# A two-layer trunk kernel rescheduled: idle products at its start, an embedding unit among the last heads, and half chunks split ahead from three tiles

## The chip, the cores and the metric

The kernel runs on one core of one Trainium2 chip. The metric is the time on the device in microseconds (us), as a median of several runs; less is better. TensorE does the matrix products (PE in the profile, its weight loads PEld), VectorE (DVE) and ScalarE (ACT) do elementwise work, GpSimd (POOL) a little, and SyncE (SP) issues the DMAs in its program order. Every engine works through its own instructions in order, and waits on semaphores for the others.

## What is computed (the reference)

Two decoder layers work on 1024 tokens of width 1024. Layer 0 mixes tokens by gated linear attention (GLA, 4 heads, chunks of 64 in the reference), layer 1 by sparse attention: an indexer of 8 small heads scores all keys, the best 256 for each query are kept, and 16 heads attend to those alone. After the mixer come a layer norm and a gated embedding. Cut to what matters:

```python
for i in range(DEPTH):                       # DEPTH = 2
    y = gla_mixer(x, ...) if i == 0 else dsa_mixer(x, ...)
    x = layer_norm(ALPHA * x + y, ln_g[i], ln_b[i])
    x = x + (p[i] @ ple_w[i]) * jax.nn.sigmoid(x @ ple_gate_w[i])

# gla_mixer                                  # dsa_mixer, for a block of 128 queries
h = x @ w_in          # q, k, v, z, a          score = sum over heads of relu(qi . ki) * wi
g = log_sigmoid(a @ w_a2 + b_a) / 16           idx = top_k(where(causal, score, -inf), 256)
G = cumsum(g)                                  probs = softmax(q . k[idx] * scale)
o = tril(q e^G . k e^-G) v + state term        o = probs @ v[idx]
y = (rmsnorm(o) * gn_g * silu(z)) @ w_out      y = (o * silu(z)) @ w_out
```

All of it is in fp32.

## The kernel before

**Products.** An fp32 product of a weight block and an activation block is made as three products of rounded parts: high by high, low by high, high by low. So every operand that TensorE reads exists as a high part (rounded by ACT) and a low part (the difference, by DVE). One product is 128x128 weights by 512 columns and goes through `mm` (L58). Which line helpers have: `split` is L403 (high, ACT) and L395 (low, DVE).

**Weights.** `Weights` holds the list of weight blocks (128x1024) in the order in which they are used. A block is loaded into a `wst` tile (L199; two of these), and split in four steps: `whi` for its two halves on ACT (L180), `wlo` on DVE (L182, or L184 with a factor). Blocks that were split earlier are loaded as `whi` and `wlo` from DRAM (L167). Steps are taken as TensorE's work is emitted, or at the latest when `take` asks for the block.

**Splitting ahead.** In the first 1030 us, the background generator `split_ahead` (L203) takes 65 weight blocks of layer 1 in 130 halves of 128x512 through: load into `pst` (L210; two tiles), high part `phi` on ACT (L219; one tile), store `whs` (L221), low part on DVE in place (L223), store `wls` (L225). The load of the next half stands on SP ahead of the store of this one's low part.

**Order of the work.** `Flow` is a clock at build time: each product adds its nominal time, and other work is put on a heap with a due time (`at`, `after`, `chain`, `spread`) or given out by three `Background` generators with a gap between steps. What is due is emitted between products. So the numbers in the code are emission times, and what they fix is the order of each engine's instructions and nothing else.

**Stages.** Both layers are gone through in two halves of 512 tokens.
- Layer 0 (until about 1030 us): for each half, four heads. `v_phase`, gates (`g_phase`: log-sigmoid as Exp then Ln on ACT, L513 and L514, then a scan on DVE, L521, and exponentials), `qk_phase`, the state recurrence, and the output products of the head before (`out_phase`). Then `tail` (L816): 8 blocks of embedding products, transposes of the normed `y`, 8 gate blocks. In half 0 follow the parts of layer 1 that need only these tokens: `small_head` (indexer's projections, tile `zz`), `small_kv` (keys, values), the indexer's scores (`ix`, `rl` L1022, `sc` L1018), and the loads of half 1's `x` (L1138).
- Layer 1: the first half begins with the same small parts of half 1. Then 16 heads, each with one or two units of other products beside it (queries `q`, gates `z`, output blocks `o`); the softmax's parts `ph` and `PT` (L1481, L1479) feed the `o` products. In half 0 the top-k searches of the later query blocks run beside the heads, as a background of counting passes (`tk<-sc,tki`, L1040 on DVE, L1084 on ACT). After head 15 come `last_outs`, three output units: (6, column half 1), (7, 0), (7, 1). The last two need `u` of head 15, which is `uf` = `o` times `z` (L1533), split by ACT and DVE. Then `norm_steps` (L789) and `tail` again.

The few lines which set what the change touches:

```python
chain((0, lambda: None), (0.6, soft(0)), (1.1, soft(1)), (0.3, scan(0)), (1.1, scan(1)), ...)   # g_phase
bg3.set(W.split_ahead(later, lp), 2.1)                    # half 0, the first head
bg3.due = max(bg3.due, fl.now + 14.0)                     # after small_head
bg.set(topk_steps([4, 5, 6, 7], scs, l1, tk, tk, on_act=(1, 2, 3)), 1.6)
```

## Time and profile before

| | |
|---|---|
| runs before | 2016.35, 2017.49, 2019.79 us; median 2017.49 |
| the profiled execution | its own time 2016.59 us; its span, from the first instruction to the last, 2014.8 us, so 1.8 us lie around the span |
| granted TensorE clock, mean | 0.993 |
| DMA | 464.96 MB, mean 231 GB/s; 16 engines busy 68.4% of the span by packets of the main queue |
| chain that ended last | PE 81%, DVE 7%, ACT 5%, DMA 4%, issue 2% |

The rows in the section below come from one profiled execution. A row of the timeline is: start in us, busy us, engine, line, operation, output<-inputs, tile shape, count, and in brackets how long the engine sat idle just before and what ended that. "DVE", "ACT" and "PE" are busy times; a matmul's busy time includes its pipeline, so products that follow each other closely overlap in their rows. A row of the waits is: who waited for whom, us in total, how often, the longest. A row of the windows is: the stretch, its length, busy time (and instructions) of PE, PEld, DVE, ACT, POOL, then the granted clock of TensorE (1 is full), the DMA engines' share and GB/s.

### The profile page before, as it was taken

Reading aid. Unit: us, or ns where it says so; the run is one execution under the profiler, and the core shown is the slowest. Engines: PE = TensorE matmul, PEld = TensorE weight load, DVE = VectorE, ACT = ScalarE, POOL = GpSimd, SP = SyncE. Lnnn points to the kernel's source line nnn. Section 1 sums busy time; section 2 is a strip of 40 time slices with the busy share of each in tenths; the row PEclk is TensorE's granted clock in tenths of the full one; section 3 lists DMA queues with packets and bytes.
Section 4 is the critical chain, followed back from the end, with each engine's and each line's share of the span. In section 5 each row is a group of like instructions: output and inputs, shape, how many; then the busy total and the mean of one; then the engine's idle time right before and its main releaser. Section 6 shows DMA issues by size and latency. Waiting matters only on the chain.

```text
span 2014.8 us, 26716 instructions
## 1 busy us (share of the span) xinstructions
PE 1963.4 (97%) x9016; PEld 1616.3 (80%) x9016; DVE 1487.6 (74%) x3037; ACT 1046.5 (52%) x1943; POOL 53.7 (3%) x111
## 2 busy tenths in 40 slices
PE   8999999999999999999999999999899999999999
PEld 6788788877777888888888887888778888888877
DVE  5667666687677797877867986777796887777863
ACT  5664646445465646464555676766442553434432
POOL 0000000010000000000100000000000000000000
PEclk9999999999999999999999999999999999999999
DMA  4557575657856565657667487877766998888864
GB/s 149 174 162 221 171 218 171 222 174 243 283 180 224 161 225 167 225 162 224 196 218 266 157 311 246 303 265 276 271 211 215 352 333 295 291 300 279 295 249 147
DMA packets 173947, 464.96 MB, mean 231 GB/s; under 512 B 20081, under 2 KB 20849, under 8 KB 167665
## 3 DMA queue, kind: packets, MB, share of 16 engines
q1 hardware_dynamic: 173808, 463.25, 68.4%
q8 instruction: 71, 1.16, 0.2%
q14 instruction: 68, 0.55, 0.1%
HBM read 331.18 MB, written 131.99 MB: 230 GB/s over the span
## 4 chain that ended last, share of the span: by engine, by line
PE 81%; DVE 7%; ACT 5%; DMA 4%; issue 2%; SPq 0%; POOL 0%; POOLq 0%; ACTq 0%; DVEq 0%
PE pb L58 59%; PE o L58 8%; PE U L58 6%; PE S L58 5%; DMA xst<-x2s 1%; DMA wls<-pst 1%; DMA pst<-in_d_o 1%; DVE bn L803 1%; PE oT L62 1%; PE tr L58 1%; DVE wlo L182 1%; DVE sc L1018 1%; ACT whi L180 0%; DMA wst<-in_g_v 0%; DMA wlo<-wls 0%
## 5 line engine op out<-in xcount | busy, mean ns | idle before, releaser
L58 PE MATMUL pb<-x,whi 128*128 128x512 f32 x2272 | 709.9, 394 | 3.3 <-ACT whi L180 2.0
L58 PEld LDWEIGHTS pb<-x,whi 128*128 128x128 f32 x2272 | 417.2, 188 | 84.4 <-ACT whi L180 2.8
L58 PE MATMUL pb<-x,wlo 128*128 128x512 f32 x1136 | 444.2, 391 | 0.4 <-DVE wlo L182 0.4
L58 PE MATMUL pb<-whi,u 128*128 128x512 f32 x1024 | 347.2, 399 | 7.6 <-DVE u L395 4.2
L58 PEld LDWEIGHTS pb<-x,wlo 128*128 128x128 f32 x1136 | 213.8, 188 | 48.1 <-DVE wlo L182 2.3
L58 PEld LDWEIGHTS pb<-whi,u 128*128 128x128 f32 x1024 | 194.8, 190 | 49.9 <-DVE u L395 5.0
L58 PE MATMUL pb<-wlo,u 128*128 128x512 f32 x512 | 202.3, 395 | 0.0
L182 DVE TENSOR_TENSOR wlo<-wst,whi 128x512 fp32r<-128x512 f32 x232 | 154.8, 684 | 56.2 <-ACT whi L180 56.0
L180 ACT ACTIVATE whi<-wst 128x512 fp32r<-128x512 f32 x232 | 136.4, 621 | 47.2 <-DMA wst<-in_g_z 13.7
L219 ACT ACTIVATE phi<-pst 128x512 fp32r<-128x512 f32 x130 | 81.4, 626 | 126.2 <-DMA pst<-in_d_z 40.8
L1435 ACT ACTIVATE sq<-P,mx 128x128 f32<-128x128 f32 (+7 forms) x128 | 99.0, 774 | 83.8 <-DVE mx L1428 56.5
L1481 ACT ACTIVATE ph<-PT 128x512 fp32r<-128x512 f32 (+1 forms) x160 | 93.7, 601 | 65.7 <-PE o L58 50.4
L58 PE MATMUL S<-kT,q 128*128 128x512 f32 (+2 forms) x576 | 121.8, 343 | 0.0
L1479 DVE TENSOR_TENSOR PT<-PT,ph 128x512 fp32r<-128x512 f32 (+1 forms) x160 | 101.5, 648 | 20.6 <-ACT ph L1481 20.6
L58 PEld LDWEIGHTS S<-kT,q 128*128 128x128 f32 x576 | 100.6, 188 | 17.8 <-DVE mx L1428 0.7
L58 PEld LDWEIGHTS pb<-wlo,u 128*128 128x128 f32 x512 | 97.6, 191 | 18.8
L223 DVE TENSOR_TENSOR pst<-pst,phi 128x512 fp32r<-128x512 f32 x130 | 89.1, 685 | 29.8 <-ACT phi L219 29.8
L1084 ACT ACTIVATE tk<-sc,tki 128x768 f16<-128x768 f32 (+2 forms) x90 | 92.9, 1032 | 22.0 <-DVE tki L1093 15.9
L58 PE MATMUL o<-ph,vT 128*128 128x512 f32 (+2 forms) x384 | 102.4, 351 | 0.0
L1441 DVE STREAM_TRANSPOSE sq<-sq 128x128 f32<-128x128 f32 (+7 forms) x128 | 97.6, 768 | 3.1 <-ACT sq L1435 3.0
L58 PE MATMUL pb<-whi,x 128*128 128x512 f32 x256 | 89.1, 407 | 10.0 <-ACT whi L180 6.0
L709 ACT ACTIVATE junk<-o 128x512 bf16<-128x512 f32 x32 | 19.1, 597 | 139.8 <-DVE ot L707 135.3
(311 smaller groups left out, 3383.9 us busy)
## 6 DMA issues: line engine op xcount, KB each, us to landing
whi<-whs SPq DMA_DIRECT2D x130, 512.0 KB
wlo<-wls SPq DMA_DIRECT2D x130, 512.0 KB
sqd<-sq SPq DMA_DIRECT2D x192, 256.0 KB
PT<-sqd SPq DMA_DIRECT2D x48, 1024.0 KB
whs<-phi SPq DMA_DIRECT2D x130, 256.0 KB
wls<-pst SPq DMA_DIRECT2D x130, 256.0 KB
wst<-in_g_v SPq DMA_DIRECT2D x32, 512.0 KB
wst<-in_g_z SPq DMA_DIRECT2D x32, 512.0 KB
```

The source lines that it names most:

```text
L58: self.pe.matmul(out, lhsT, rhs, start=start, stop=stop)
L62: self.pe.transpose(out, in_, ident)
L180: self.nc.scalar.activation(hi[:, c], st[:, c], AF.Copy, scale=1.0 if gain is None else gain)
L182: self.nc.vector.tensor_sub(lo[:, c], st[:, c], hi[:, c].bitcast(F32))
L219: self.nc.scalar.activation(hi, st.bitcast(F32), AF.Copy)
L223: self.nc.vector.tensor_sub(st, st.bitcast(F32), hi.bitcast(F32))
L803: dve.bn_stats(st8[:, t, c], y[:, t, c * 512:c * 512 + 512])
L1084: act.activation(junk()[:, :n], scs[j], AF.Sign, bias=cand[:, j:j + 1].bitcast(F32), accum_out=cnt[:, j:j + 1])
L1435: act.activation(to, rows, AF.Exp, scale=-1.0, bias=mx, accum_out=sm[:, t:t + 1])
L1441: dve.transpose(x, x)
L1479: dve.tensor_sub(lo, lo.bitcast(F32), hi.bitcast(F32))
L1481: chain((0, lambda: act.activation(hi, lo.bitcast(F32), AF.Copy)), (0.8, second))
```

## The change

1. **Start.** 22 products `ident` by `ident` (128x128, fp32, result unused) stand ahead of TensorE's first product. The first block's four split steps and the split of the first `x` block are emitted one after the other, then the rest.
2. **Gates.** `g_phase` takes Exp of both halves, then Ln of both; the scans are put 2.2 us later and 0.7 us apart.
3. **Splitting ahead.** Three `pst` tiles, and the loads run two halves ahead instead of one; `phi` takes turns in the two `xst` tiles of another pool; gap 2.06 instead of 2.1. From the start of `small_head`, the generator is held for seven blocks (35.8 us by the build clock), so nothing of it stands beside the indexer's blocks; before, it was held for 14 us after `small_head`.
4. **Half 1's `x`** is loaded by its own generator during `small_head`, two blocks each 5 us, and is split later and more slowly (from block 12 of `small_kv`, gap 2.2). The first weights of half 1 (`in_g_v`) are no longer tied to these loads.
5. **Layer 0's end of a half.** The inputs of the embedding are staged in the `e1` tile and split 7 us later.
6. **Norm.** The statistics of the first 512 columns are taken as soon as these are complete; the apply step comes at 1.8 instead of 2.0.
7. **Layer 1's end of a half.** Two of the eight embedding blocks (12 products) become a unit of `last_outs` between (6, 1) and (7, 0), with weights in the `wst` tiles; the tail does the other six. `z` times `inv` is taken one group earlier. In half 1, head 15's `o` products are packed into 4.2 us. The embedding's inputs are loaded at head 14 instead of head 15, and the searches pause 5 us after head 15's last group.
8. **Searches.** Gap 1.52 (was 1.6), and in the heads' slots 1.75 or 1.5.

The diff's core:

```diff
     def split_ahead(self, keys, pool, hi_pool):
...
-            st = pool.tile([128, 512], F32R, tag="pst", name="pst", bufs=2)
+                tiles[i] = pool.tile([128, 512], F32R, tag="pst", name="pst", bufs=3)
...
+        load(0)
+        load(1)
...
-            hi = pool.tile([128, 512], F32R, tag="phi", name="phi")
+            hi = hi_pool.tile([128, 512], F32R, tag="xst", name="phi", bufs=2)
...
-            nxt = load(*cuts[i + 1]) if i + 1 < len(cuts) else None
+            load(i + 2)
...
-    last_outs = [("o", (6,), 1), ("o", (7,), 0), ("o", (7,), 1)]
+    last_outs = [("o", (6,), 1), ("p",), ("o", (7,), 0), ("o", (7,), 1)]
...
+        def exps():
+            for d in range(2):
                 act.activation(ta[:, d], ta[:, d], AF.Exp, scale=-1.0)
+
+        def logs():
+            for d in range(2):
                 act.activation(ta[:, d], ta[:, d], AF.Ln, bias=1.0)
...
+            fl.need(lambda: X.t[0] is not None)
+            for _ in range(4):
+                W.step()
             next(feeder)
             feed_by(feeder, 0.0, 0.0)
+            idle = pp.tile([128, 512], F32, tag="o", name="o")
+            for _ in range(22):
+                nc.tensor.matmul(idle[:, 0:128], ident, ident, start=True, stop=True)
...
-                    bg3.set(W.split_ahead(later, lp), 2.1)
+                    bg3.set(W.split_ahead(later, lp, xp), 2.06)
...
+            nxt = start_half(1)
+            feed_by(nxt[3], fl.now + 2.0, 5.0)
+            bg3.due = max(bg3.due, fl.now + 7 * B)
             fl.run(small_head(0, X, f32t, alloc, lambda: t2k("u", F32R), tmp, ups, kih, kil, res))
...
-            bg3.due = max(bg3.due, fl.now + 14.0)
-            nxt = start_half(1)
-            next(nxt[2])
...
+                if g == len(groups) - 2:
+                    z, inv = get(("z", h), ("inv", h))
+                    dve.tensor_mul(z, z, inv)
+                    st["zs", h] = z
                 if last:
-                    dve.tensor_mul(z[0], z[0], z[1])
...
-        bg.set(topk_steps([4, 5, 6, 7], scs, l1, tk, tk, on_act=(1, 2, 3)), 1.6)
+        bg.set(topk_steps([4, 5, 6, 7], scs, l1, tk, tk, on_act=(1, 2, 3)), 1.52)
...
+    def ple_unit(st):
+        st["pw"] = W.take(("p", 1, 0))
+        st["ple"] = [small_tile("qf") for _ in range(2)]
+        for b in range(2):
+            yield from ple_block(st["pw"], b, Pt, st["ple"][b], act)
...
+            bg.gap = 1.75 if h > 3 and h % 4 < 2 else 1.5
```

What that does to the order of the instructions is shown at three places.

**ACT, the gates of the first head** (`z` is a block of the output gate, `ta` the gate's halves). Before:

```order
L602 ACT_TABLE_LOAD
L602 ACTIVATE z<-pb 128x512
L513 ACT_TABLE_LOAD
L513 ACTIVATE ta<-ta 128x512
L514 ACT_TABLE_LOAD
L514 ACTIVATE ta<-ta 128x512
L180 ACTIVATE whi<-wst 128x512
L513 ACT_TABLE_LOAD
L513 ACTIVATE ta<-ta 128x512
L514 ACT_TABLE_LOAD
L514 ACTIVATE ta<-ta 128x512
```

The same place after the change:

```order
L610 ACT_TABLE_LOAD
L610 ACTIVATE z<-pb 128x512
L519 ACT_TABLE_LOAD
L519 ACTIVATE ta<-ta 128x512 x2
L181 ACTIVATE whi<-wst 128x512
L523 ACT_TABLE_LOAD
L523 ACTIVATE ta<-ta 128x512 x2
```

Four table loads for a head's Exp and Ln have become two; the weights' `whi` stands between the pairs.

**SP, the indexer's blocks of half 0** (`in_x_T` is half 1's raw `x`, `in_g_v` its first weights, `in_d_q` a half to be split ahead). Before:

```order
L225 DMA wls<-pst 128x512
L221 DMA whs<-phi 128x512
L210 DMA pst<-in_d_q 128x512
L1138 DMA y<-in_x_T 128x512
L199 DMA wst<-in_g_v 128x1024
L1138 DMA y<-in_x_T 128x512
L199 DMA wst<-in_g_v 128x1024
L1138 DMA y<-in_x_T 128x2x512 x3
L963 DMA v<-rope_s 32x512
L964 DMA v<-rope_s 32x512
L199 DMA wst<-in_g_v 128x1024 x2
L225 DMA wls<-pst 128x512
```

After:

```order
L1160 DMA y<-in_x_T 128x2x512
L168 DMA whi<-whs 128x1024
L168 DMA wlo<-wls 128x1024
L1160 DMA y<-in_x_T 128x2x512
L985 DMA v<-rope_s 32x512
L986 DMA v<-rope_s 32x512
L200 DMA wst<-in_g_v 128x1024 x3
L230 DMA wls<-pst 128x512
L200 DMA wst<-in_g_v 128x1024
L226 DMA whs<-phi 128x512
L214 DMA pst<-in_d_q 128x512
```

The loads of `x` stand apart and ahead of the weights, and no `phi` or `pst` stands between them and `in_g_v`.

**PE and SP, the end of layer 1's half 0** (`o` are head 15's last groups, `pb<-whi,u` output products, `pb<-q,wst` the embedding unit, `sc` the indexer's scores of the query blocks that are still searched). PE before:

```order
L58 MATMUL o<-PT,vT_9801 128x4x96
L58 MATMUL pb<-whi,u 128x512
L58 MATMUL pb<-wlo,u 128x512
L58 MATMUL pb<-whi,u 128x512
L58 MATMUL o<-ph,vT_9801 128x4x64
L58 MATMUL o<-ph,vT_9802 128x4x64
L58 MATMUL o<-PT,vT_9801 128x4x64
L58 MATMUL o<-ph,vT_9801 128x4x64
L58 MATMUL o<-ph,vT_9802 128x4x64
L58 MATMUL o<-PT,vT_9801 128x4x64
L58 MATMUL pb<-whi,u 128x512
L58 MATMUL pb<-wlo,u 128x512
```

PE after:

```order
L58 MATMUL o<-PT,vT_9821 128x4x96
L58 MATMUL pb<-q,wst 128x512 x3
L58 MATMUL o<-ph,vT_9821 128x4x64
L58 MATMUL o<-ph,vT_9822 128x4x64
L58 MATMUL o<-PT,vT_9821 128x4x64
L58 MATMUL o<-ph,vT_9821 128x4x64
L58 MATMUL o<-ph,vT_9822 128x4x64
L58 MATMUL o<-PT,vT_9821 128x4x64
L58 MATMUL pb<-q,wst 128x512 x6
L58 MATMUL pb<-whi,u 128x512
L58 MATMUL pb<-wlo,u 128x512
```

SP before:

```order
L1507 DMA inv<-row 128x512
L1077 DMA sc_9809<-sc_s 128x768
L167 DMA whi<-whs 128x1024
L167 DMA wlo<-wls 128x1024
L1077 DMA sc_9810<-sc_s 128x896
L1077 DMA sc_9811<-sc_s 128x1024
```

SP after:

```order
L1099 DMA sc_9829<-sc_s 128x768
L1536 DMA inv<-row 128x512
L1099 DMA sc_9830<-sc_s 128x896
L168 DMA whi<-whs 128x1024
L168 DMA wlo<-wls 128x1024
L1099 DMA sc_9831<-sc_s 128x1024
```

In place of the first three output products, embedding products stand between the last `o` groups, and six more behind the last. The scores of 896 keys are loaded ahead of a pair of weight blocks instead of behind it.

More of the change, by code (lines that the diff above doesn't have):

```diff
@@ L163, in step @@
                 self.loads(n + 1)
-            self.parts[n] = tuple(self.pool.tile([128, 1024], F32R, tag=t, name=t, bufs=4) for t in ("whi", "wlo"))
+            tags = (("wst", 2),) * 2 if self.seq[n][0][:3] == ("p", 1, 0) else (("whi", 4), ("wlo", 4))
+            self.parts[n] = tuple(self.pool.tile([128, 1024], F32R, tag=t, name=t, bufs=b) for t, b in tags)
         if whole:
@@ L773, in out_phase @@
             parts = [W.take(("o", u["h"], ch, 0)), W.take(("o", u["h"], ch, 1))]
-            for i, _ in enumerate(accumulate(parts, U, y, ch, u["rs"], norm if ch else None)):
+            for i, _ in enumerate(accumulate(parts, U, y, ch, u["rs"], norm)):
                 if ch:
@@ L810, in apply, with ple_block, tail @@
                 f_done[t] = True
-            chain((0, stats), (2.0, apply))
+            if ch:
+                chain((0, stats), (1.8, apply))
         return norm, f_done
-    def tail(layer, Pt, y, y_done, final, tp, xps, x_alloc, tmp):
-        ple = [tp.tile([128, 4, HT], F32, tag="z", name="ple", bufs=2) for _ in range(2)]
+    def ple_block(parts, b, Pt, out, engine):
+        hi, lo = parts
+        ps = pbank()
+        n = 0
+        for k in range(2):
+            ph, pl = Pt[k]
+            bs = slice(k * 512 + b * 128, k * 512 + b * 128 + 128)
+            for l, r in ((hi, ph), (hi, pl), (lo, ph)):
+                mm(ps, l[:, bs], r, n == 0, n == 5)
+                n += 1
+            if k == 0:
+                yield
+        if engine is dve:
+            dve.tensor_copy(out, ps)
+        else:
+            act.activation(out, ps, AF.Copy)
+        yield
+    def tail(layer, Pt, y, y_done, final, tp, xps, x_alloc, tmp, ple=(), first=None):
+        ple = list(ple)
+        done = len(ple)
+        for c in range(2):
+            t = tp.tile([128, 4, HT], F32, tag="z", name="ple", bufs=2)
+            ple += [t[:, i] for i in range(4)]
         X1 = [None] * NK
@@ L1138, in load, with fetch @@
             nc.sync.dma_start(raw[:, k:k + n], x_T[k:k + n, :, hs].rearrange("k p t -> p k t"))
+        def fetch():
+            for k in range(0, NK, 2):
+                load(k, 2)
+                yield
         def feed():
-            load(0, 1)
-            W.loads(W.ns + 1)
-            load(1, 1)
-            W.loads(W.ns + 2)
-            for k in range(2, NK, 2):
-                load(k, 2)
-            if half == 0:
+            if half == 0:
+                load(0, 1)
+                W.loads(W.ns + 1)
+                load(1, 1)
+                W.loads(W.ns + 2)
+                for k in range(2, NK, 2):
+                    load(k, 2)
                 nc.sync.dma_start(ba, g_ba)
@@ L1151, in feed @@
                 nc.sync.dma_start(fq, freq)
-            else:
-                yield
             for k in range(NK):
@@ L1512, in f @@
             def f():
-                (ph, pl), *z = get(("parts", h, g), *([("z", h), ("inv", h)] if last else []))
+                (ph, pl), = get(("parts", h, g))
                 fl.req(not first or st.get("done", -1) == h - 1, not last or h < 5 or st["out"] >= h - 4)
@@ L1644, in trunk_kernel @@
                 spread(parts[early:], start + lead + early * step, dur - lead - 2.4 - early * step)
-                spread(pvs, start + lead + 2.9, dur - lead - 2.4)
+                if h == 15 and half:
+                    spread(pvs, start + 8.6, 4.2)
+                else:
+                    spread(pvs, start + lead + 2.9, dur - lead - 2.4)
             if h < 15:
```

112 lines of the change are left out of this document (52 added, 60 removed).

## The prediction

> **What bounds the kernel now.** I read the page's first parts, then the windows by stage, the waits of TensorE, and the timeline around each window in which TensorE idles.
>
> ```profile
> PE 1963.4 (97%) x9016; PEld 1616.3 (80%) x9016; DVE 1487.6 (74%) x3037; ACT 1046.5 (52%) x1943; POOL 53.7 (3%) x111
> ...
> 0.00:12.43 12.43, 5.47 (x11) 3.71 (x12) 5.93 (x14) 7.72 (x13) 2.37 (x12) 1.00 0.76 264
> ...
> 405.00:425.00 20.00, 17.95 (x81) 14.54 (x80) 15.25 (x26) 9.43 (x23) 1.79 (x6) 0.91 0.32 105
> ...
> 530.00:566.00 36.00, 29.77 (x117) 22.90 (x116) 31.07 (x56) 22.82 (x43) 0.00 (x0) 0.91 0.65 220
> ...
> 630.00:650.00 20.00, 16.79 (x73) 13.75 (x73) 14.00 (x34) 7.34 (x16) 0.75 (x2) 0.91 0.82 289
> 650.00:1220.00 570.00, 564.88 (x2632) 466.49 (x2631) 460.36 (x985) 325.71 (x612) 19.23 (x39) 1.00 0.63 210
> 1220.00:1240.00 20.00, 17.84 (x76) 14.37 (x75) 14.58 (x36) 11.22 (x25) 0.00 (x0) 0.91 0.77 282
> ...
> 1440.00:1462.00 22.00, 15.87 (x63) 12.49 (x62) 14.68 (x27) 3.87 (x7) 0.00 (x0) 0.84 0.80 281
> ...
> 1930.00:1950.00 20.00, 17.94 (x72) 14.07 (x71) 13.75 (x24) 4.62 (x9) 0.39 (x2) 0.91 0.65 256
> ```
>
> TensorE is busy 97% of the span, and its products are what the work consists of: in 650 to 1220 it idles 5.12 us of 570. So only three things can be won: the first 6 us, the holes, and the clock. Six short stretches hold nearly all of that. Their idle time is 20 - 17.95 = 2.05, 36 - 29.77 = 6.23, 20 - 16.79 = 3.21, 20 - 17.84 = 2.16, 22 - 15.87 = 6.13 and 20 - 17.94 = 2.06 us. In each, the granted clock is below 1, and I looked for where:
>
> ```profile
> 411.79:415.20 3.41, 3.41 (x12) 2.75 (x11) 3.14 (x6) 0.00 (x0) 0.00 (x0) 0.50 0.27 71
> ...
> 1452.85:1459.68 6.83, 4.24 (x10) 3.37 (x11) 5.35 (x10) 0.00 (x0) 0.00 (x0) 0.50 0.73 258
> 1940.96:1944.37 3.41, 3.41 (x8) 2.76 (x9) 1.43 (x3) 0.00 (x0) 0.00 (x0) 0.50 0.00 0
> ```
>
> Behind each hole lies a window of 3.41 us at half clock; these three rows stand for seven such stretches, of which the second holds two windows. One in which TensorE is busy throughout costs at most 3.41 / 2 = 1.7 us. There are two in 530 to 566 and two in 1440 to 1462 (there with 4.24 us busy, so 2.1 us together). What is to be had at most is thus 3.8, 9.6, 4.9, 3.9, 8.2 and 3.8 us: 34.2 in all, and the start.
>
> **The change part by part.** *Start.*
>
> ```profile
> 1.09 0.23 DVE L356 TENSOR_SCALAR ident<-negs 128x128 f32<-128x128 int32 x1 [1.09 <-POOL negs L354]
> ...
> 5.98 0.79 PE L58 MATMUL pb<-whi,x 128*128 128x512 f32 x1 [5.98 <-ACT whi L180]
> ...
> 7.74 1.29 DVE L395 TENSOR_TENSOR x<-y,x 128x512 fp32r<-128x512 f32 x2
> ...
> 9.92 1.05 PE L58 MATMUL pb<-whi,x 128*128 128x512 f32 x2
> ...
> 10.78 0.63 PE L58 MATMUL pb<-wlo,x 128*128 128x512 f32 x1
> ...
> 12.46 0.39 PE L58 MATMUL pb<-whi,x 128*128 128x512 f32 x1
> ...
> 12.69 0.40 PE L58 MATMUL U<-whi,x 128*128 128x512 f32 x1
> ...
> 15.45 0.39 PE L58 MATMUL pb<-whi,x 128*128 128x512 f32 x1
> ...
> 95.89 0.45 PE tr L58 x4
> ```
>
> The first weight block's 24 products last from 5.98 to 15.45. Three take 10.78 - 9.92 = 0.86 us until 12.43, that is, 0.43 each (though this window's row says 1.00, so I take the slow pace from the products), and 0.23 behind it. The idle products can begin at 1.32, when `ident` is there. 128x128 products of this kind take 0.45 / 4 = 0.112 us (last row); 22 at half pace take 4.9 us and end at about 6.3, no later than the first product's operands by more than 0.3. If the pace is full by 9, the sixth product, which needs `x` 1's low part at about 8.9 (DVE's second half of the row at 7.74, behind two `wlo`), is what comes last. The 18 behind it then take 18 x 0.23 = 4.1, and end at 13.0: 2.4 us gained. If it stays slow until 12.43, 0.7.
>
> *Gates.*
>
> ```profile
> L513 ACT ACT_TABLE_LOAD x16 | 20.5, 1283 | 0.3
> ...
> PE pb L58 <- DVE m L509: 3.0, 6, 0.8
> ```
>
> There are as many for Ln at L514, and half of the 32 go: 16 x 1.283 = 20.5 us of ACT, which is 52% busy, so nearly all of it lies beside TensorE's work. What TensorE feels is its wait for the gates, 3.0 us in six times. I take 2.0 (0 to 3.0), and with the start 4.4.
>
> *405 to 425.* TensorE waits for `Al`, the low part of the chunk's scores:
>
> ```profile
> 407.15 0.62 ACT L219 ACTIVATE phi<-pst 128x512 fp32r<-128x512 f32 x1
> ...
> 407.81 0.69 DVE L223 TENSOR_TENSOR pst<-pst,phi 128x512 fp32r<-128x512 f32 x1 [1.84 <-ACT phi L219]
> ...
> 411.34 0.50 PE L58 MATMUL o<-v,Al 128*128 128x512 f32 x1 [2.05 <-DVE Al L395]
> ```
>
> A half's `phi` stands on ACT just ahead of `Ah`, and its `pst` ahead of DVE's queue that ends in `Al`. With other gaps, they stand behind: 0.62 + 0.69 of the 2.05 us go, likely the window with it. I take 2.8 (0 to 3.8).
>
> *530 to 566.* The indexer's blocks:
>
> ```profile
> 542.08 1.15 ACT L180 ACTIVATE whi<-wst 128x512 fp32r<-128x512 f32 x2 [4.27 <-DMA wst<-in_g_v]
> ...
> 543.66 0.62 PE L58 MATMUL ix<-v,u 128*128 128x384 f32 x2 [2.51 <-ACT rl L1022]
> ...
> 561.54 0.75 PE L62 MATMUL U<-ident,zz 128*128 128x128 f32 x4 [2.81 <-ACT zz L984]
> ```
>
> ACT waits 4.27 us at a weight half that was issued among the loads of `x`; `rl` and TensorE behind it stop for 2.51. The loads of `x` now lie earlier and apart, nothing else is ahead of the weights, and that hole closes with its window. The second, 2.81, comes from DVE, which is busy 31.07 of these 36 us; one `x` split (0.69) more or less stands there, and a `pst` has come into it. I take 5.0 (2.5 to 8.0).
>
> *630 to 650.* A `phi` holds ACT:
>
> ```profile
> ACT phi L219 <- DMA pst<-in_d_z: 40.8, 19, 4.1
> ...
> 633.28 0.33 SPq L210 DMA_DIRECT2D pst<-in_d_o  x1
> ...
> 637.08 0.63 ACT L219 ACTIVATE phi<-pst 128x512 fp32r<-128x512 f32 x1 [3.29 <-DMA pst<-in_d_o]
> ...
> 637.74 0.69 DVE L223 TENSOR_TENSOR pst<-pst,phi 128x512 fp32r<-128x512 f32 x1 [1.81 <-ACT phi L219]
> ...
> 639.09 0.49 PE L58 MATMUL tr<-ta,m 128*128 128x128 f32 x2 [3.21 <-DVE m L589]
> ```
>
> The load lands 3.8 us after its issue, the `phi` waits 3.29 at the head of ACT, DVE 1.81 behind it, TensorE 3.21 behind that. ACT's next `whi` stands behind that `phi` too. A load now comes a whole half earlier, three steps of 2.06 = 6.2 us, which covers 3.29. On SP it stands between the same two stores as before and waits for the same one (the low part of the half before), so nothing queued behind it waits longer; the `phi` waits for the store of the last but one instead of the last. I take 4.4 (0, if SP is what holds the load, to 4.9).
>
> *1220 to 1240.* Here, DVE does a counting pass and its search step between the operands and `PT`:
>
> ```profile
> 1225.41 0.84 DVE L1040 TENSOR_SCALAR_CACHE_REDUCE tk<-sc,tki 128x640 f16<-128x640 f32 x1
> ...
> 1229.94 0.50 PE L58 MATMUL o<-PT,vT 128*128 128x512 f32 x1 [2.16 <-DVE PT L1479]
> ```
>
> With other gaps, the pass no longer stands right ahead of this `PT`. I take 2.8; bounds 3.9, and below nothing the same price again (-3.9), since denser passes can come to stand so at another head.
>
> *1440 to 1462.*
>
> ```profile
> 1448.36 0.69 DVE L1524 TENSOR_TENSOR z<-z,inv 128x512 f32<-128x512 f32 x1
> ...
> 1450.56 0.50 PE L58 MATMUL pb<-whi,u 128*128 128x512 f32 x1 [1.98 <-ACT u L403]
> ...
> 1452.43 1.15 DVE L1040 TENSOR_SCALAR_CACHE_REDUCE tk<-sc,tki 128x896 f16<-128x896 f32 x1 [2.58 <-DMA sc<-sc_s]
> ...
> 1455.44 1.22 PE L58 MATMUL pb<-whi,u 128*128 128x512 f32 x2 [4.15 <-DVE u L395]
> ```
>
> Two holes. The first is the way from the last `o` to `u`'s high part (`z`, `uf`, `u`: 0.69 + 0.69 + 0.63); the second is a count that waits 2.58 us on DVE for its scores, ahead of `u`'s low part. Now 6 + 9 products stand behind the last `o`, 15 x 0.23 = 3.5 us, against `uf`, `u`, `u` = 0.69 + 0.63 + 0.69 = 2.0. The count still stands ahead of `uf`, but its scores are loaded ahead of a weight pair. I take 6.8 (3.0, if the count's wait stays, to 8.2).
>
> *1930 to 1950* is the same without the count: 18 products, 4.1 us, against 2.0. I take 2.8 (1.0 to 3.8). The two embedding blocks are only moved; the tail's transposes have 24 products ahead of them instead of 30, for which I put 0.6 on the other side.
>
> *New holes.* Every gap has another value, so background steps stand elsewhere in 1700 us which now idle little. One hole like that at 1227 is likely: 2.16 + 1.7 = 3.9.
>
> The sum: 4.4 + 2.8 + 5.0 + 4.4 + 2.8 + 6.8 + 2.8 - 0.6 - 3.9 = 24.5. The profiled execution took 2016.6, which is 0.9 below the median of the runs, within their scatter; 2016.6 - 24.5 = 1992.1. By its bounds this case reaches from 1984 to 2002.
>
> The Trainium skill, in TensorE: Matmul & The Clock Gate, section HAM oscillation, warns of idle gaps over some 3.4 us alone. Here holes of 2.05 and 2.16 us are followed by windows at 0.50, so the trace says that shorter ones do it too; by the page, the windows would have other causes.
>
> **The rivals.**
> *The windows at half clock stay* (that page's rule): only the idle time is won. In what I took, that is about 1.2 us at each of four holes, 1.7 at 540 and 2.1 at 1450, or 8.6: 24.5 - 8.6 = 15.9, so 2001. For it: the holes were short. Against: no window lies away from a hole.
> *Half of each hole stays*: the loads still queue behind the weights on SP and on the DMA engines (share 0.82 at 630 to 650), the indexer's stretch is bound by DVE (31.07 of 36), and behind each wait that goes the next one is only a little earlier. Then 24.5 / 2 = 12, so 2004.
> *The searches hurt (slower)*: passes at 1.5 instead of 1.6, in ten heads' slots, stand ahead of `PT` on DVE, each time for 3.9 us. From 24.5 / 3.9, between six and seven such slots, the gain is eaten; with eight, 2016.6 - 24.5 + 31.2 = 2023. Against: there was one such hole in sixteen slots, and six slots get 1.75.
> *It doesn't do what it says*: the idle products take four passes (0.43 x 22 = 9.5 us, first product at 10.8, 4.8 lost), and `pst` still waits: gains at 1440 and 1930 (9.6) against 4.8 and 3.9 lost, so about 2016.
>
> **How the numbers follow.** Forecast 0.55, half-clock windows 0.10, half of the holes 0.23, no gain 0.06, searches 0.06. The likeliest gives 1992. The range takes in the forecast's bounds and both smaller gains, and leaves out the last two: 1984 to 2010. About 0.2%, 4 us, is what a measurement can tell. Faster by more 0.88, within 0.05, slower 0.07.
>
> **What would show it.** In the profile after: the first real product near 6 with 0.23 from product to product by 9; 16 table loads at Exp and Ln together; no wait of TensorE over 2 us around 409, 543, 637, 1450; `phi` waiting for `pst` well below 40.8 us; windows at 0.50 gone where holes are gone. The prediction is wrong if TensorE's idle time outside the start falls by less than 10 us, or if `o` waits for `PT` in several heads.

## The result, and the profile after

The changed kernel takes 1988.63 us (median of four runs, 1987.37 to 1989.54), the kernel before 2018.64 (four runs, 2016.35 to 2022.6): a ratio of 0.9849, with a 95% interval of 0.9831 to 0.9867. The profiled execution took 1987.81 us, its span is 1986.0 us against 2014.8, and the mean granted clock is 0.998 against 0.993. Forecast were 1992 us; the gain on the profiled executions is 28.8 us where 24.5 were summed up.

The windows of the changed kernel, each laid over about the same work as the window of before (9 to 25 us earlier by the clock; columns as before; the second row stands for 12.43 to 95 us of before):

```profile
0.00:13.49 13.49, 12.12 (x69) 11.15 (x69) 6.67 (x16) 8.13 (x14) 2.30 (x12) 1.00 0.74 250
13.49:91.00 77.51, 76.71 (x345) 63.13 (x344) 52.54 (x89) 47.28 (x76) 0.75 (x2) 1.00 0.49 169
396.00:416.00 20.00, 19.89 (x94) 15.49 (x93) 17.54 (x31) 12.11 (x26) 2.23 (x6) 1.00 0.45 134
515.00:551.00 36.00, 32.82 (x136) 25.78 (x135) 32.03 (x58) 23.84 (x45) 0.00 (x0) 0.91 0.56 185
611.00:631.00 20.00, 20.00 (x97) 16.61 (x96) 13.93 (x35) 8.75 (x20) 0.75 (x2) 1.00 0.90 297
1201.00:1221.00 20.00, 20.00 (x97) 16.80 (x96) 16.73 (x44) 13.00 (x28) 0.00 (x0) 1.00 0.85 285
1418.00:1440.00 22.00, 20.55 (x91) 16.28 (x91) 17.89 (x34) 3.91 (x7) 0.75 (x2) 1.00 0.74 282
...
1905.00:1926.00 21.00, 20.75 (x92) 16.41 (x91) 15.06 (x26) 3.48 (x6) 2.19 (x5) 1.00 0.66 254
```

Five of the six holes are closed, or nearly, and the clock is full there: in the six stretches TensorE idled 21.8 us in all, and idles 5.0 now. What remains is the indexer's stretch (515 to 551): TensorE idles 3.18 us, and the only two windows at half clock ahead of the last instructions lie in it. DVE is busy 32.03 of its 36 us.

Where the time came from is seen when the same product is looked up in both traces, at places where neither runs at half clock. Seven of TensorE's products in the timeline of before:

```profile
90.83 0.50 PE L58 MATMUL U<-v,kh 128*128 128x512 f32 x1 [0.86 <-ACT kh L660]
...
498.92 0.62 PE L58 MATMUL pb<-S,whi 128*128 128x512 f32 x2
...
600.73 0.61 PE L58 MATMUL pb<-x,whi 128*128 128x512 f32 x2
...
800.19 0.39 PE L58 MATMUL U<-wlo,x 128*128 128x512 f32 x1
...
1100.14 0.74 PE L58 MATMUL S<-kI,ix 128*128 128x256 f32 x4
...
1402.09 0.27 PE L62 MATMUL S<-ident,sm 128*4 128x128 f32 x1 [1.73 <-DVE sm L1487]
...
1600.21 0.27 PE L62 MATMUL S<-ident,sm 128*4 128x128 f32 x1
```

The same seven in the timeline of the changed kernel:

```profile
82.85 0.39 PE L58 MATMUL U<-v,kh 128*128 128x512 f32 x1
...
487.48 0.62 PE L58 MATMUL pb<-S,whi 128*128 128x512 f32 x2
...
584.96 0.62 PE L58 MATMUL pb<-x,whi 128*128 128x512 f32 x2
...
779.37 0.39 PE L58 MATMUL U<-wlo,x 128*128 128x512 f32 x1
...
1081.81 0.74 PE L58 MATMUL S<-kI,ix 128*128 128x256 f32 x4
...
1378.99 0.27 PE L62 MATMUL S<-ident,sm 128*4 128x128 f32 x1
...
1571.90 0.27 PE L62 MATMUL S<-ident,sm 128*4 128x128 f32 x1
```

The differences are 7.98, 11.44, 15.77, 20.82, 18.33, 23.10 and 28.31 us, and 28.8 at the end. So the stretches between them gained:

| stretch, by before's times | forecast | gained |
|---|---|---|
| start and first gates, to 91 us | 4.4 | 8.0 |
| to 499 (`Al`, 409) | 2.8 | 3.5 |
| to 601 (indexer's blocks) | 5.0 | 4.3 |
| to 800 (`phi`, 637) | 4.4 | 5.1 |
| to 1100 (layer 0's last head and tail) | none | -2.5 |
| to 1402 (`PT`, 1227) | 2.8 | 4.8 |
| to 1600 (last outputs and tail of half 0) | 6.5 | 5.2 |
| to the end (the same of half 1) | 2.5 | 0.5 |
| new holes somewhere | -3.9 | in the rows above |

One row is a loss. The changed kernel's waits of TensorE from 915 to 995 us hold one for the residual sums `y` that before does not have there, and at 1297 one for `sm` is new:

```profile
PE pb L58 <- DVE y L768: 0.7, 2, 0.4
...
1297.48 0.27 PE L62 MATMUL S<-ident,sm 128*4 128x128 f32 x1 [0.87 <-DVE sm L1516]
```

So new holes did come, small ones: 2.5 us are lost by 1100 us and 1.0 at 1297. What the change does to layer 0's end of a half and to the norm (points 5 and 6) lies where the 2.5 are lost; the prediction had no term for these points, and no run took them apart.

In the changed kernel's groups of instructions on ACT, the table loads of Exp (L519) and Ln (L523), and the splits ahead:

```profile
L224 ACT ACTIVATE phi<-pst 128x512 fp32r<-128x512 f32 x130 | 80.5, 619 | 0.4 <-DMA pst<-in_d_q 0.4
...
L519 ACT ACT_TABLE_LOAD x8 | 10.3, 1283 | 0.1
L523 ACT ACT_TABLE_LOAD x8 | 10.3, 1283 | 0.1
```

16 of 32 table loads are gone, as counted. And ACT, which idled 126.2 us ahead of a `phi` before, idles 0.4 us there: the loads two ahead are always there.

### The profile page after: what moved, and what is told of

It is laid out like the page before. It is cut to its first block, busy times and chain, and to the rows that moved or that the text cites. A ratio compares the mean times of both kernels' runs of the same rounds, so it can differ in the third digit from the quotient of the medians.

```text
span 1986.0 us, 26826 instructions
## 1 busy us (share of the span) xinstructions
PE 1958.4 (99%) x9060; PEld 1613.9 (81%) x9060; DVE 1490.3 (75%) x3037; ACT 1021.6 (51%) x1927; POOL 52.1 (3%) x111
## 4 chain that ended last, share of the span: by engine, by line
PE 83%; DVE 8%; ACT 3%; DMA 3%; issue 2%; SPq 1%; POOL 0%; POOLq 0%; DVEq 0%; ACTq 0%
PE pb L58 62%; PE o L58 8%; PE S L58 6%; PE U L58 5%; DVE bn L809 1%; ACT x L859 1%; PE oT L62 1%; PE tr L58 1%; DVE y L770 1%; DMA xst<-x2s 1%; DVE sc L1040 1%; DVE wlo L183 0%; DVE y L768 0%; DMA wls<-pst 0%; DMA wst<-in_ple_c 0%
## 5 line engine op out<-in xcount | busy, mean ns | idle before, releaser
L58 PE MATMUL pb<-whi,u 128*128 128x512 f32 x1024 | 342.9, 395 | 0.5 <-DVE y L770 0.5
L58 PE MATMUL U<-whi,x 128*128 128x512 f32 x256 | 84.3, 390 | 0.0
```

The costliest lines, as they stand in the source:

```text
L58: self.pe.matmul(out, lhsT, rhs, start=start, stop=stop)
```

## The experiments

Each kernel is the changed kernel with one edit, unless it says otherwise. The times are medians; the kernel before, run beside them, took 2017.2 to 2019.1 us. The changed kernel's 1988.63 was not run again beside them, so differences of a microsecond or so rest on the traces and not on the times. The traces scatter too, above all at the start: in nine executions whose first 14 us are the same instructions (the 22 idle products among them), the second weight block starts at 13.32 to 14.79 us. So what arises in the first 14 us counts for nothing below where the edit comes later.

### The idle products left out

```diff
-            idle = pp.tile([128, 512], F32, tag="o", name="o")
-            for _ in range(22):
-                nc.tensor.matmul(idle[:, 0:128], ident, ident, start=True, stop=True)
```

Expected: 

> The changed kernel without the 22 idle products; all else as in the changed kernel. My theory (the idle products bring the granted pace to full before the first real product): without them the first product starts near 6, the first 24 products take 0.43 us apart until a window edge, and the second weight block starts about 2 us later than in the changed kernel, so about 1990.6 us. Rival (the order of the first splits gained it, the idle products nothing): the second block starts at 13.5 or earlier, time within 0.5 us of 1988.6 or below it, since the idle products themselves end only at 7.9.

Measured: 1990.03 us (1988.78 to 1991.35), a ratio of 0.9864 (0.9845 to 0.9883). First the changed kernel's own start:

```profile
1.37 6.80 PE L1215 MATMUL o<-ident 128*128 128x128 f32 x44 [1.37 <-DVE ident L362]
7.93 0.47 PE L58 MATMUL pb<-whi,x 128*128 128x512 f32 x1
...
13.49 0.39 PE L58 MATMUL pb<-whi,x 128*128 128x512 f32 x1
```

Then the start without idle products:

```profile
6.21 0.80 PE L58 MATMUL pb<-whi,x 128*128 128x512 f32 x1 [6.21 <-ACT whi L181]
...
8.81 1.05 PE L58 MATMUL pb<-whi,x 128*128 128x512 f32 x2
9.67 0.63 PE L58 MATMUL pb<-wlo,x 128*128 128x512 f32 x1
...
14.38 0.39 PE L58 MATMUL pb<-whi,x 128*128 128x512 f32 x1
```

Without them, two products take 0.86 us (8.81 to 9.67) until 11.4 us; with them, the products run at full pace from the first. The second weight block (the last row of each) starts at 14.38 instead of 13.49, so between these two traces the idle products are worth 0.9 us, and the order of the splits the other 15.45 - 14.38 = 1.1 us of the start. Neither figure is safe: other executions with the 22 products start that block at up to 14.79 us, and another execution of the kernel before's start has it at 17.10 instead of 15.45. What is shown is the pace: the first block's 24 products take 5.5 to 5.9 us in all nine executions with the 22 idle products, and 8.2 without. The time that this saves is partly given back, since the first product starts later (7.93 instead of 6.21). The 22 products show as 44 records: one takes twice what I had put.

### Fourteen idle products, with the embedding back in the tail

```diff
-            for _ in range(22):
+            for _ in range(14):
```

Expected: 

> The embedding unit back in the tail, and 14 idle products instead of 22, which end at about 6.3 us by the rows of the changed kernel (16 at 0.213 us, then 0.112), when the first operands are there. My theory (the last eight idle products are pure delay, but x 1's low part at 8.4 limits the first block): the second weight block starts 0.4 to 0.8 us earlier than at 13.5, time 1986.3 to 1986.7 us. Rival (the clock falls back in the wait that opens behind the fewer idle products): the first block slower, 1988 us or more.

(From the kernel with the embedding unit back in the tail, the experiment further below.)

Measured: 1985.83 us (1985.44 to 1987.46), ratio 0.9851 (0.9837 to 0.9866). In its timeline, the fourth product waits for `x` 1's high part:

```profile
8.38 0.50 PE L58 MATMUL pb<-whi,x 128*128 128x512 f32 x1 [0.80 <-ACT x L409]
```

The first real product starts at 6.17 instead of 7.93, but the second weight block at 13.54 instead of 13.49. The expected 0.4 to 0.8 us are not there in this trace, in which `x` 1's parts came late. They are in the other trace with 14 idle products, that of the last experiment: 12.77. So the data sets the first block's end, and whether the last eight cost anything is open. This kernel's time is 1.2 us below that of the kernel it is made from (1987.07); it had one window at half clock at 544 us instead of two, and none at 1428, where that one had one; nothing ties this to the edit.

### Exp and Ln of each half after each other again

```diff
-        def exps():
-            for d in range(2):
+        def soft(d):
+            def f():
                 act.activation(ta[:, d], ta[:, d], AF.Exp, scale=-1.0)
-
-        def logs():
-            for d in range(2):
                 act.activation(ta[:, d], ta[:, d], AF.Ln, bias=1.0)
+            return f
...
-        chain((0, lambda: None), (0.6, exps), (1.2, logs), (2.2, scan(0)), (0.7, scan(1)),
-              (1.0, middle), (1.9, decays))
+        chain((0, lambda: None), (0.6, soft(0)), (1.1, soft(1)), (0.3, scan(0)), (1.1, scan(1)),
+              (0.8, middle), (1.9, decays))
```

Expected: 

> The changed kernel with Exp and Ln of each gate half after each other again (four table loads a head instead of two) and the old spacing of the scans. Between 57 and 91 us the changed kernel is 6.4 us ahead of the kernel before. My theory (table loads on ACT delayed the weights' high parts there): this kernel falls back by 5 to 7 us before 100 us, and by 1 more at later heads: about 1995 us. Rival (the ordering of background work moved by the other edits made it): under 2 us, below 1991 us.

Measured: 1996.21 us (1995.43 to 1996.58), ratio 0.9895 (0.9873 to 0.9917), so 7.6 us slower. Two of its products:

```profile
63.28 0.73 PE L58 MATMUL pb<-x,whi 128*128 128x512 f32 x2 [1.14 <-ACT whi L181]
...
89.81 0.73 PE L58 MATMUL U<-v,kh 128*128 128x512 f32 x2 [0.99 <-ACT kh L666]
```

The product that the changed kernel starts at 82.85 starts at 89.81 here: 7.0 us of the 7.6 are lost before 90 us. The wait for a weight's high part (63.28) stands as it did before at 64.42. My theory holds: in the first head, where ACT also makes the rope tables and splits the weights just in time, the two more table loads delay the weights themselves. At the other heads the loads lie beside TensorE's work. The edit puts the scans back at their old spacing too, and the run doesn't tell that part from the table loads.

### Splitting ahead as before: two tiles, one ahead

```diff
-                tiles[i] = pool.tile([128, 512], F32R, tag="pst", name="pst", bufs=3)
+            st = pool.tile([128, 512], F32R, tag="pst", name="pst", bufs=2)
...
-            hi = hi_pool.tile([128, 512], F32R, tag="xst", name="phi", bufs=2)
+            hi = pool.tile([128, 512], F32R, tag="phi", name="phi")
...
-            load(i + 2)
+            nxt = load(*cuts[i + 1]) if i + 1 < len(cuts) else None
```

Expected: 

> The changed kernel with the old way of splitting ahead: two pst tiles, a phi tile of its own, the next half loaded one ahead; gap and pause of the changed kernel stay. My theory (the load of a half lands too late by 3 us at some places, and two ahead covers it): ACT waits for pst by 30 us or more in all instead of few, and TensorE has 4 to 8 us of new holes in 95 to 1030 us: 1993 to 1997 us. Rival (the one hole at 637 went because the steps of the background moved, not for the tiles): ACT's waits for pst grow but no hole over 1 us appears, within 1.5 us of 1988.6.

Measured: 1994.05 us (1992.4 to 1996.14), ratio 0.9884 (0.9865 to 0.9904), so 5.4 us slower. A row of the groups on ACT:

```profile
L219 ACT ACTIVATE phi<-pst 128x512 fp32r<-128x512 f32 x130 | 81.5, 627 | 127.3 <-DMA pst<-in_d_q 29.8 <-DMA pst<-in_d_o 25.5 <-DMA pst<-in_d_z 23.9
```

And the hole in the timeline:

```profile
451.19 0.63 ACT L219 ACTIVATE phi<-pst 128x512 fp32r<-128x512 f32 x1 [3.66 <-DMA pst<-in_d_z]
...
452.54 1.11 PE L62 MATMUL U<-ident,y 128*128 128x128 f32 x4 [3.57 <-ACT x L855]
```

ACT's idle time ahead of `phi` is back at 127.3 us. The hole is not back at 637 but stands in layer 0's tail, with two windows at half clock behind it: a late load holds ACT for 3.66 us, and TensorE for 3.57 behind that. By the same products, this place costs 5.2 us. So the mechanism is shown, and its place is a matter of where a late load happens to meet an ACT step that TensorE needs.

### Halves split beside the indexer's blocks again

```diff
-            bg3.due = max(bg3.due, fl.now + 7 * B)
...
+            bg3.due = max(bg3.due, fl.now + 14.0)
```

(The second line stands behind `small_head`, as before the change.)

Expected: 

> The changed kernel, but halves are split ahead beside the indexer's blocks again, with the old pause of 14 us behind small_head; x of half 1 is still loaded early. My theory (the indexer's stretch is bound by DVE, and the hole at 540 came from the weight in_g_v queued behind loads): the stretch gets 1 to 2.5 us longer, for two to three pst subtractions of 0.69 us on DVE and their loads, about 1990 us. Rival (the pause is what closed the hole): 4 us or more, 1993 us or above.

Measured: 2000.45 us (1998.77 to 2001.45), ratio 0.9915 (0.9896 to 0.9934), so 11.8 us slower, the largest of all, and my theory's 1 to 2.5 us are far off. SP's waits from 505 to 545 us:

```profile
SPq L214 <- DMA wls<-pst: 16.3, 4, 5.8
```

The timeline of the same stretch:

```profile
527.70 0.33 SPq L214 DMA_DIRECT2D pst<-in_d_q  x1
...
529.52 7.99 SPq L200 DMA_DIRECT2D wst<-in_g_v  x3
...
535.19 1.15 ACT L181 ACTIVATE whi<-wst 128x512 fp32r<-128x512 f32 x2 [11.02 <-DMA wst<-in_g_v]
...
536.77 1.01 PE L58 MATMUL ix<-v,u 128*128 128x384 f32 x2 [7.02 <-ACT rl L1044]
```

A half's load into a `pst` tile waits on SP until the store from that tile has landed: 16.3 us in four waits. What is queued behind it on SP waits too, and here that is `in_g_v`, issued at 529.52 and not at 515.3 as in the changed kernel. ACT stands 11.02 us at it, TensorE 7.02. The loads of `x` were early in this kernel as well. So it is the pause of splitting, not the early `x`, that closed the hole at 540. But the 11.8 us are not what the pause gained: the whole change gained 4.3 us in this stretch, and by the same products this run loses 10 there, so it is worse than the kernel before. With the same pause of 14 us, SP waited only 8.3 us in two such waits over the same work before the change. So the pause is needed because of the other edits, of which the loads two ahead are the likeliest; what it would do in the kernel before was not run.

### Half 1's `x` loaded in one go again

```diff
-            feed_by(nxt[3], fl.now + 2.0, 5.0)
...
+            for _ in nxt[3]:
+                pass
```

(The new lines stand behind `small_head`.)

Expected: 

> The changed kernel, but half 1's x is loaded in one go behind small_head, as before, and splitting ahead pauses as in the changed kernel. My theory (after the run with splits beside the indexer: what counts is that in_g_v isn't held on SP behind the stores of splits): the loads of x, 2 MB, delay in_g_v by their transfer alone, a hole of 2 to 4 us at 530 with its window, 1991 to 1994 us. Rival (the pause alone does it): within 1 us of 1988.6.

Measured: 1989.91 us (1989.44 to 1990.49), ratio 0.9864 (0.9847 to 0.9881). It lies 1.1 us behind the changed kernel at 123 us already, ahead of the edit, and 1.6 to 1.7 at 551. The edit itself costs about 0.6 us: the rival is right.

### The searches at the old gap

```diff
-        bg.set(topk_steps([4, 5, 6, 7], scs, l1, tk, tk, on_act=(1, 2, 3)), 1.52)
+        bg.set(topk_steps([4, 5, 6, 7], scs, l1, tk, tk, on_act=(1, 2, 3)), 1.6)
...
-            bg.gap = 1.75 if h > 3 and h % 4 < 2 else 1.5
```

Expected: 

> The changed kernel with the searches' steps at the old gap of 1.6 throughout. My theory (the hole at 1227 was one unlucky place of a counting pass ahead of PT; the finer gaps only place the passes otherwise): the passes come to stand ahead of PT at one or two heads between 1120 and 1400 us, 2 to 5 us in all, about 1992 us. Rival (the gaps do nothing, the hole went because the other edits moved the heads): within 1 us of 1988.6. Third (denser passes cost elsewhere): faster than 1987.

Measured: 1992.26 us (1992.05 to 1993.87), ratio 0.9878 (0.9863 to 0.9892), so 3.6 us slower. Its two new holes:

```profile
1213.67 0.50 PE L58 MATMUL o<-PT,vT 128*128 128x512 f32 x1 [2.14 <-DVE PT L1508]
...
1384.84 0.27 PE L62 MATMUL S<-ident,sm 128*4 128x128 f32 x1 [2.33 <-DVE sm L1516]
```

These are the holes that before had at 1229.94 and 1402.09, at the same products, with 2.16 and 1.73 us. So the gaps took both away. By the same products, 2.0 us of this trace's 4.4 arise ahead of the searches, where the edit does nothing; the two holes cost 2.4 and 2.5, and 2.4 come back, 1.0 of them at 1297, where the changed kernel's new wait for `sm` is gone. So the edit costs 2.5, which lies in my theory's 2 to 5, and the holes come back at the places that they had before, with the old gap.

### The searches' new gaps alone, in the kernel before

```diff
-        bg.set(topk_steps([4, 5, 6, 7], scs, l1, tk, tk, on_act=(1, 2, 3)), 1.6)
+        bg.set(topk_steps([4, 5, 6, 7], scs, l1, tk, tk, on_act=(1, 2, 3)), 1.52)
...
+            bg.gap = 1.75 if h > 3 and h % 4 < 2 else 1.5
```

Expected: 

> The kernel before with one edit: the searches' gaps (1.52, then 1.75 or 1.5 in the heads' slots). My theory (the gaps only place the passes; at 1227 they take one out of PT's way, while at the end of half 0 the earlier inputs and z times inv were needed too): the hole at 1227 goes (3 to 4 us), and at 1450 a count of 1024 keys, whose scores still land late, takes the place of the one of 896, so that hole stays: 2014 us against 2017.5. Rival (the gaps made both gains): both holes go, 9 to 12 us, 2007 us. Third (the place of passes is luck in each kernel): a hole appears elsewhere between 1120 and 1440 and the time is that of before within 2 us.

Measured: 2014.84 us (ten runs, 2011.38 to 2018.22), ratio 0.9984 (0.9974 to 0.9994). The windows at the two places:

```profile
1221.00:1241.00 20.00, 20.00 (x97) 16.83 (x96) 16.73 (x42) 13.23 (x30) 0.00 (x0) 1.00 0.79 283
1439.00:1461.00 22.00, 18.85 (x73) 14.30 (x72) 18.50 (x38) 3.87 (x7) 0.69 (x2) 0.84 0.80 282
```

The hole at 1227 is closed by this edit alone. The one at 1450 shrinks from 6.13 to 3.15 us of idle time, because the scores of 896 keys now come ahead of a weight pair (the new gaps alone do that); the rest of it needs the other edits. With the start put aside, which is 1.7 us later in this trace with the same instructions, the edit gains 3.9 us at 1227 and 1.9 at 1402.

### The embedding unit back in the tail

```diff
...
-    last_outs = [("o", (6,), 1), ("p",), ("o", (7,), 0), ("o", (7,), 1)]
+    last_outs = [("o", (6,), 1), ("o", (7,), 0), ("o", (7,), 1)]
...
-                        tp, spsum, lambda k: (next(gx), next(gx)), tmp1, *first)
+                        tp, spsum, lambda k: (next(gx), next(gx)), tmp1)
```

Expected: 

> The changed kernel with the embedding unit back in the tail, all eight blocks there; z times inv one group earlier, the earlier loads and the packed o products of head 15 stay. My theory (the 12 products cover the way from the last o to u): two holes come back, each of 0.7 to 1.5 us with a window at half clock behind it, one at the end of each half, and the tails gain about 1 us each from 30 products of cover: net 2 to 5 us, 1990.6 to 1993.6 us. Rival (the earlier loads and the earlier z times inv had closed the holes alone): within 1 us of 1988.6, or faster.

Measured: 1987.07 us (1986.7 to 1987.25), ratio 0.985 (0.9835 to 0.9865). The intervals overlap, but all four runs lie below all four of the changed kernel. The wait that comes back:

```profile
1427.66 0.65 PE L58 MATMUL pb<-whi,u 128*128 128x512 f32 x1 [0.89 <-ACT u L409]
```

It is 0.89 us instead of the 1.98 and 4.15 of before, with one window at half clock, and the tail, which has its 30 products of cover again, gives that back. The unit is worth nothing. The gain at 1450 thus doesn't come from the cover. What is left is the order of the loads, which the run with the gaps alone shows, and `z` times `inv` one group earlier, which no run took apart.

### The embedding's inputs late again (unit in the tail)

```diff
-            if h == 14:
-                Pt = load_p(1, half, lambda: small_tile("q", F32R, 4), dur + 2.5,
+            if h == 15:
+                Pt = load_p(1, half, lambda: small_tile("q", F32R, 4), 14.0,
```

Expected: 

> The embedding in the tail (22 idle products), and its inputs loaded and split at head 15 again, as before the change, so that the split of q stands between uf and u's low part, and the two loads ahead of the scores of 768 keys. My theory (after the unit turned out to be worth nothing, the earlier inputs and the scores loaded ahead of a weight pair closed the holes at 1450): the split of q alone costs 1.29 us ahead of u in half 0, with a window, 1 to 3 us: 1988 to 1990 us. Rival (the order of the scores' load alone closed them): within 0.6 us of 1987.1. Third (the inputs were all of it): 4 us or more, 1991 us.

Measured: 1988.01 us (1987.87 to 1988.84), ratio 0.9862 (0.9847 to 0.9876), 0.9 us more than the kernel that it is made from, which is at the lower edge of my theory and outside the rival's 0.6. The traces show next to nothing at the end of half 0: the wait for `u`'s high part is 0.90 us against 0.89 without the edit, though the split of `q` stands ahead of `u`'s low part. By the same products, 0.6 us arise in small steps before 1548 us, and 0.5 more by 1914. So the rival (the order of the scores' loads) holds for half 0, and in half 1 the late inputs cost some 0.5 us at most.

### Holes put in on purpose

```diff
+            if half and h in (0, 2, 4, 6, 8, 10, 12):
+                hp, ht = pbank(), negs
+                nc.tensor.matmul(hp[:, 0:128], ident, ident, start=True, stop=True)
+                act.activation(ht, hp[:, 0:128], AF.Copy)
+                for _ in range((0, 3, 5, 7, 9, 12, 15)[h // 2]):
+                    pool.memset(ht, 0.0)
+                hq = pbank()
+                nc.tensor.matmul(hq[:, 0:128], ht, ident, start=True, stop=True)
```

Expected: 

> The changed kernel with seven holes put into TensorE's work between units of layer 1's half 1, made by a chain of 0, 3, 5, 7, 9, 12 and 15 memsets of 0.2 us on GpSimd between two small products: holes of about 1.3 to 4.5 us. My theory (a hole of 2 us or more is followed by a window of 3.41 us at half clock): windows at 0.50 behind the longer five or so, none behind the shortest. Rival (only holes longer than a window of 3.41 us lower the clock): windows behind the last two at most.

Measured: 2015.77 us in the profiled execution; the holes, from the start of one small product to that of the next, are 1.04, 1.43, 2.01, 2.53, 3.06, 3.84 and 4.62 us. The stretches at half clock of this run begin at 1677.19, 1731.81, 1793.25 and 1851.27, that is, behind the last four, on one grid of 3.41 us. The windows ahead of them and behind, by PE's busy time and the clock:

```profile
1673.78:1677.19 3.41, 1.50 (x8) 1.29 (x9) 2.06 (x5) 0.65 (x2) 1.43 (x7) 1.00 1.03 418
1677.19:1680.60 3.41, 3.41 (x12) 3.02 (x11) 1.70 (x6) 0.61 (x1) 0.00 (x0) 0.50 0.99 413
...
1844.45:1847.86 3.41, 1.61 (x11) 1.29 (x9) 1.95 (x5) 1.65 (x4) 1.08 (x6) 1.00 0.83 287
1847.86:1851.27 3.41, 0.86 (x5) 0.78 (x6) 0.65 (x1) 0.00 (x0) 1.98 (x10) 1.00 1.01 410
1851.27:1854.68 3.41, 3.41 (x12) 3.03 (x11) 0.56 (x2) 0.00 (x0) 0.00 (x0) 0.50 1.00 415
```

In this run, a window of the grid with 1.50 us busy (1.91 idle) is followed by one at half clock, one with 1.61 us busy (1.80 idle) is not. So what counts is how much of one window the hole fills. A hole of 2.53 us lowered the clock, and one of 2.01 us, which fell over a window's edge at 1619.17 (1.37 us idle in the window behind it), did not. My theory's threshold of 2 us is near, its rule was not: in the run with the old gaps, holes of 2.53 and 2.72 us from product to product brought no window at all.

### Loads behind the store, and a longer pause

From the kernel with the embedding in the tail and 14 idle products:

```diff
             self.nc.sync.dma_start(there[0][:, c], hi.bitcast(F32))
-            load(i + 2)
             self.nc.vector.tensor_sub(st, st.bitcast(F32), hi.bitcast(F32))
             yield
             self.nc.sync.dma_start(there[1][:, c], st.bitcast(F32))
+            load(i + 2)
...
-            bg3.due = max(bg3.due, fl.now + 7 * B)
+            bg3.due = max(bg3.due, fl.now + 9 * B)
```

Expected: 

> As the kernel with the embedding in the tail and 14 idle products, and besides: a half's load is issued behind the store of this half's low part instead of ahead of it, and the pause of splitting ahead is nine blocks instead of seven. My theory (SP stands at the load until the store before has landed, 103.5 us in 59 waits in the changed kernel, and what is queued behind it comes late; the pst at 543 is in the hole at 541): these waits of SP fall under 30 us, and the hole at 541 with its two windows gets smaller by 1 us or more: 1983 to 1986 us. Rival (none of these waits reaches TensorE, since the weights are two blocks ahead, and the hole at 541 is DVE's scores): within 0.7 us of the kernel it starts from.

Measured: 1983.36 us (1982.73 to 1986.3), ratio 0.9842 (0.9826 to 0.9859); mean granted clock 1.000. SP's waits at the loads:

```profile
SPq L214 <- DMA wls<-pst: 5.1, 4, 1.9
```

The hole in the indexer's stretch, in the timeline:

```profile
543.04 0.66 PE L62 MATMUL U<-ident,zz 128*128 128x128 f32 x4 [1.88 <-ACT zz L1006]
```

SP's waits fall from 99.5 us in the kernel that it starts from (103.5 in the changed one) to 5.1, as expected, but the hole is the same 1.88 us (1.87 in the changed kernel). It stands where ACT and TensorE wait for DVE's scores (with one low part of `x` among them), and the splits of halves have no part in it. The windows at half clock behind it are gone in this run, since the hole lies otherwise on the grid. Of the 2.5 us against the kernel it starts from, 1.1 are there before 14 us, where the edit does nothing yet; 1.0 more by 555 us, around the windows at half clock that are gone, and 0.8 between there and 993 us, where halves are still split (0.2 come back later). Two edits were made at once, so which of them did this stays open. This is the fastest of these kernels, below the changed one by its median (5.3 us) and by all its runs; the intervals of the ratios overlap.

## Why the prediction was right, point by point

- **What bounds the kernel** was right: TensorE's busy time fell by 5 us only (1963.4 to 1958.4, with 6.8 us of idle products in the latter), the span by 28.8. The gain is the holes and the clock. TensorE's idle time outside the start fell by 18 us (44.4 to 26.2), where less than 10 was to be the sign of a wrong prediction. One reading was wrong: the six stretches do not hold nearly all of the idle time, but 21.8 of 51.4 us, and the start 7.0. Of the rest, 4.6 lay in the stretch of the first gates:

```profile
12.43:95.00 82.57, 77.96 (x335) 61.53 (x334) 51.55 (x87) 46.76 (x70) 0.00 (x0) 1.00 0.42 141
```

- **Start**: 2.4 forecast, 1.96 between the two traces, and wrong inside. I took the row `PE tr x4` for four products; those are four records, and an fp32 product of 128 columns leaves two. The idle products end at 7.9 and not at 6.3. Since executions with the same start differ by up to 1.7 us, the agreement is partly luck. The rival in which they take four passes had the direction, not the size.
- **Gates**: the term that was mis-sized. I read its price off TensorE's waits for the gates themselves (3.0 us) and took 2.0. The stretch gave 6.0 behind the start, its idle time fell from 4.61 to 0.80 us, and the run with Exp and Ln apart costs 7.6. The table loads hold ACT, and behind ACT stood the weights' high parts (the waits for `whi` at 60 and 64 us), `kh`, and all that follows in the first head. The rows for this were in the trace of before, and the mean of 52% misled: from 40 to 70 us, ACT was busy 25.9 of 30 us.
- **405 to 425**: 3.5 for 2.8 in its stretch. No run took it apart from the rest.
- **530 to 566**: 4.3 for 5.0, the cause half right. That the weight queued on SP was what came last is shown; that the earlier loads of `x` freed it is not: they give about 0.6. Without the pause of splitting, the kernel is 11.8 us slower.
- **630 to 650**: 5.1 for 4.4, and shown: without the third tile and the second load ahead, ACT's idle time ahead of `phi` is 127.3 us and a hole of 3.57 us with two windows returns, elsewhere.
- **1220 to 1240**: 4.0 at this hole by the same products, for 2.8, and 1.9 at a hole at 1402 that had no term; both are shown in both directions by the gaps of the searches. A new wait at 1297 took 1.0 back.
- **1440 to 1462, 1930 to 1950**: 5.2 and 0.5 with the tails, for 6.5 and 2.5. The cover of 15 and 18 products, on which I had built both terms, is worth nothing: the tails lose what it gains. The count's wait for its scores is gone, as forecast:

```profile
1425.28 1.14 DVE L1062 TENSOR_SCALAR_CACHE_REDUCE tk<-sc,tki 128x896 f16<-128x896 f32 x1
...
1426.35 0.68 DVE L1567 TENSOR_TENSOR uf<-o,z 128x512 f32<-128x512 f32 x1
```

- **New holes**: 3.9 was put as one hole like that at 1227. None of that size came, but the small ones at 880 to 1010 us and at 1297 cost 3.5 in all, so the sum needed the term, for another reason than the one given.
- **The range**: the bounds of the forecast, 1984 to 2002, are not the sums of the terms' bounds. With each term at its worst, the new hole among them, these give 2018.
- **The sum**: 24.5 for 28.8. The 4 us that the gates gave beyond their term make the difference; the other rows miss by 0.4 to 2.0 each, and these misses nearly cancel.
- **The rivals**: the windows at half clock went with the holes, so the rival in which they stay is out. Half of each hole did not stay: of 21.8 us, 5.0 are left. The searches cost nothing; they gained.

## What to carry to other kernels

When an in-order engine is held by something short (a table load, a late tile, a DMA wait on the issuing queue), price it by everything that is queued behind it on that engine, not by the waits that name it: here 1.3 us loads on an engine that is half idle over the whole run cost 7 us in one head, where it was busy 86% of the time. A background that loads, splits and stores needs its tiles free before its load is issued, because the queue that issues the load carries others' transfers too. And a group of fixes should be taken apart once it is done: one of these (the embedding unit) was worth nothing, and a small one (the pause) could not be left out without losing 11.8 us. A gain is best read from the same product in both traces, at places with full clock: read inside a slow window, it hides what is lost between.

## What the runs showed of the hardware

- The granted clock falls to half for one or two windows of a fixed 3.41 us grid after a window in which TensorE idled more than about half. In these traces (the program's first 20 and last 10 us aside), every window with 1.87 us idle or more was followed by half clock. Below, from 1.66 us on, some were (1.79, 1.72, and 1.66 at one place in two kernels) and some were not (1.80, 1.72, 1.70); from a window at full clock, 1.53 us and less never was. The Trainium skill, in TensorE: Matmul & The Clock Gate, section HAM oscillation, names idle gaps over about 3.4 us; the holes put in here lowered the clock from 2.53 us on.
- An fp32 product of 128x128 by 128 columns leaves two records, in the changed kernel 0.213 us apart at the start and 0.112 from 4.8 us on: the 22 products took 6.56 us. In two other executions the pace rose at 7.35 and 7.57 us only, and the first real product came at 9.14 and 9.25.
- An activation table load took 1.283 us in every row.
